# Gate and up weights of the second layer stored with their columns interleaved, and loaded with a stride

## The chip, the cores and the metric

The kernel runs on one core of one Trainium2 chip. The time is device microseconds of one execution, and the number compared is the median of several executions. TensorE does the matrix products: it loads 128 weight columns from SBUF and then streams a moving operand past them into PSUM. VectorE and ScalarE do elementwise work, SyncE issues most of the transfers.

## The reference, cut to what matters

One inference step of a two-layer decoder: 256 prompt tokens and 8 x 4 sample tokens share the weights, so 288 columns of activations in all. Each layer has a mixer (a retention and RG-LRU mixer in the first layer, an S5 state-space mixer with a GLU in the second) and then a SwiGLU feed-forward part:

```python
def swiglu(x, w_gu, w_down):
    h = x @ w_gu
    g, u = jnp.split(h, 2, axis=-1)
    return (jax.nn.silu(g) * u) @ w_down
...
            x = x + swiglu(rmsnorm(x, norm_ffn[layer]), w_ffn_gu[layer], w_ffn_down[layer])
```

`D_MODEL` is 2048 and `FFN_HIDDEN` 5632. All inputs are float32.

## The kernel before, in words

Activations lie with the 128 feature channels of a chunk on the partitions and the 288 tokens along the free dimension; 2048 features are 16 chunks. A weight matrix is stored by `_tiles` as tiles of 128 output columns: tile `t` is an array of 128 partitions by 2048, whose columns `128 k` to `128 k + 127` are the weights of chunk `k`.

The large products run in float32r. To keep accuracy, each float32 operand is split in two parts, a rounded one (`wh`, `xh`) and the rest (`wl`, `xl`), and each chunk takes three products: `wh` with `xh` (L328), `wh` with `xl` (L329), `wl` with `xh` (L330). Every product is one weight load (128 columns) and one pass over 288 columns of activations.

The program is a list of units, written out in order by `even_mixer`, `glu` and `ffn`. A `Unit` is one tile of output columns over the chunks `k0` to `k1`; `run_prog` plays the list. Each unit is cut in two halves, and each half (up to 8 chunks) has a weight slot of up to 1024 columns. For a slot, SyncE issues one transfer into `raw` (L274), ScalarE copies it to `wh` in float32r (L281), VectorE subtracts to get `wl` (L109, the helper of all tensor-tensor operations), and then TensorE runs the products of that half. There are four `raw` and four `wh` buffers, and three or four `wl` buffers, so these steps run ahead of TensorE by up to three slots. Chunk `k` is read as `wh[:, o:o + P]`, 128 neighbouring columns.

`ffn(l, ...)` takes the 44 tiles of the hidden width in three thirds, 0 to 14, 15 to 29 and 30 to 43 (`THIRDS`). In a third, each tile `t` has a gate unit and an up unit of 16 chunks each; then 16 units of the down projection follow. Gate and up results are evacuated from PSUM by VectorE and ScalarE (`evg`, `evu`). The activations of the second layer's feed-forward part are in the tiles `x` of the pool `x2`.

Other places that the text speaks of: L748 (`cross_sum`), products of 128 weight columns with 32 moving columns in float32; L533 (`lru_gate`), products with 312 moving columns in float32; and the VectorE operations of `yl_evac`, `gr_evac` and `rot_units`, where one operand (`hs` or `rot`) is read or written with a step of 4 elements for the prompt tokens, and in `yl_evac` with a step of 7 elements for the 32 sample tokens.

Of the kernel before, what the change touches and what calls it, by code (L numbers as in the profile page):

```python
# [19 lines left out]
P = 128  # L20
D = 2048
NT = D // P
# [7 lines left out]
NH = HID // P  # L30
# [10 lines left out]
V_BG = 96  # L41
V_CW, V_CB, V_BA, V_BX, V_LAM = 128, 160, 168, 176, 184
V_N = 192


@with_exitstack
def trunk_kernel(ctx: ExitStack, tc: tile.TileContext, ins, outs, upto=99, dbg=None):
    nc = tc.nc
    v, act, pe, pool, sp = nc.vector, nc.scalar, nc.tensor, nc.gpsimd, nc.sync
# [11 lines left out]
    def nm(s):  # L61
        cnt[0] += 1
        return f"{s}{cnt[0]}"

    def g_(w=N, p=P):
        return AP_["gen"].tile([P, TOK], F32, tag="g", name=nm("g"))[:p, :w]
# [24 lines left out]
    def mp_():  # L91
        return AP_["ps"].tile([P, 512], F32, tag="m", name=nm("mp"))
# [15 lines left out]
    def tt(o, a, b, op):  # L108
        v.tensor_tensor(o, a, b, op=op)  # L109
# [7 lines left out]
    def stt(o, a, s, b, op0, op1):  # L117
        v.scalar_tensor_tensor(o, a, s, b, op0=op0, op1=op1)
# [11 lines left out]

    vec = cst.tile([P, V_N], F32, name="vec")
    sp.dma_start(vec, ins["vec"])
# [12 lines left out]
    def later(n, fn):  # L145
        pend.append((step[0] + n, len(pend), fn))

    def run_due():
        due = [p for p in pend if p[0] <= step[0]]
        for p in due:  # L150
            pend.remove(p)
        for p in due:
            p[2]()
        if bgq:
            bg_one()
# [54 lines left out]
        return h, l  # L210

    class Unit:
        __slots__ = ("w", "k0", "k1", "rhs", "evac", "late")

        def __init__(self, w, k0, k1, rhs, evac, late=0):
            self.w, self.k0, self.k1, self.rhs, self.evac, self.late = w, k0, k1, rhs, evac, late

    prog = []
    S = {}
# [1 line left out]
    def unit(*a):  # L221
        prog.append(Unit(*a))

    def call(fn):
        prog.append(fn)

    def halves_of(u):
        m = u.k0 + (u.k1 - u.k0 + 1) // 2
        return [(u, u.k0, m), (u, m, u.k1)]

    def run_prog():
        ws, items, where, left = [], [], {}, []

        def slot(*pieces):
            o = 0
            for u, a, b in pieces:
                for k in range(a, b):
                    where[id(u), k] = (len(ws), a - o)
                o += b - a
            ws.append(pieces)  # L240
            left.append(o)
        lead = [u for u in prog if isinstance(u, Unit)][:4]
        for u in prog:
            if isinstance(u, Unit):
                if u in lead[1:]:
                    continue
                hs = [halves_of(x) for x in (lead if u is lead[0] else (u,))]
                for e in range(2):
                    for h in hs:
                        items.append(h[e])  # L250
                        slot(h[e])
            elif isinstance(u, tuple):
                for pieces in u[0]:
                    slot(*pieces)
                items.extend(u[1])
            else:
                items.append(u)
        accs = {}
        raws, whs, wls = {}, {}, {}
        S["whs"] = whs  # L260
        n = len(ws)
        LH, RAW = 3, 4
        for tag in ("raw", "wh"):
            wt.tile([P, 1024], F32R if tag == "wh" else F32, tag=tag, name=nm(tag))
        wt.tile([P, 32], F32, name="wpad", bufs=1)
        ring = [wt.tile([P, 1024], F32R, name=f"wl{k}", bufs=1) for k in range(3)]
        free = S["free"] = list(ring)
        size = [k * P for k in left]

        def dma(i):  # L270
            r = wt.tile([P, 1024], F32, tag="raw", name=nm("raw"), bufs=RAW)
            o = 0
            for u, a, b in ws[i]:
                sp.dma_start(r[:, o:o + (b - a) * P], u.w[:, a * P:b * P])  # L274
                o += (b - a) * P
            raws[i] = r

        def prep_h(i):
            w = size[i]
            wh = wt.tile([P, 1024], F32R, tag="wh", name=nm("wh"), bufs=LH + 1)  # L280
            act.activation(wh[:, :w], raws[i][:, :w], AF.Copy)  # L281
            whs[i] = wh

        def prep_l(i):
            w = size[i]
            wl = free.pop(0)
            tt(wl[:, :w], raws.pop(i)[:, :w], whs[i][:, :w].bitcast(F32), SUB)
            wls[i] = wl

        c = [0, 0, 0]  # L290
        done = 0

        def dma_next():
            dma(c[0])
            c[0] += 1

        def prep_next():
            prep_h(c[1])
            c[1] += 1

        def prepl_next():
            prep_l(c[2])
            c[2] += 1

        start(dma_next, prep_next, prepl_next)
        for h in items:
            while True:
                while c[0] < min(c[2] + RAW, n):
                    dma_next()
                while c[1] < min(c[0], done + LH + 1, n):  # L310
                    prep_next()
                if c[2] >= done + 3 or c[2] >= n:
                    break
                prepl_next()
            if not isinstance(h, tuple):
                h()
                continue
            u, a, b = h
            i, w0 = where[id(u), a]
            if a == u.k0:  # L320
                bank = mp_() if u in lead else psa.tile([P, 512], F32, tag="acc", name=nm("acc"))
                accs[id(u)] = (bank[:, :N], u.rhs())
            acc, rhs = accs[id(u)]
            wh, wl = whs[i], wls[i]
            for k in range(a, b):
                o = (k - w0) * P
                xh, xl = rhs[k - u.k0]
                pe.matmul(acc, lhsT=wh[:, o:o + P], rhs=xh, start=(k == u.k0), stop=False)  # L328
                pe.matmul(acc, lhsT=wh[:, o:o + P], rhs=xl, start=False, stop=False)  # L329
                pe.matmul(acc, lhsT=wl[:, o:o + P], rhs=xh, start=False, stop=(k == u.k1 - 1))  # L330
            if b == u.k1:
                if u in lead or u.late:
                    later(u.late or 3, lambda u=u, acc=acc: u.evac(acc))
                else:
                    u.evac(acc)
            left[i] -= b - a
            if left[i] == 0:
                whs.pop(i)
                free.append(wls.pop(i))
                assert i == done  # L340
                done += 1
                step[0] += 1
                run_due()
# [3 lines left out]
    xs = {}  # L347
# [603 lines left out]
    def ffn(l, fin):  # L951
        for a, b in THIRDS:
            hid = {}
            for t in range(a, b):
                st = {}

                def evg(ps, st=st):
                    g, t_ = g_(), g_()
                    tt(g, ps, rstd["v"], MUL)
                    act.activation(t_, g, AF.Tanh, scale=0.5)  # L960
                    st["g"], st["t"] = g, t_

                def evu(ps, st=st, t=t, hid=hid):
                    u = g_()
                    tt(u, ps, rstd["v"], MUL)
                    stt(st["g"], st["t"], 1.0, st["g"], ADD, MUL)
                    tt(u, u, st["g"], MUL)
                    hid[t] = split(u, 0.5, ac_, al_)
                late = 2 if t < 1 else 0
                unit(ins["w_gu"][l, t], 0, NT, lambda: xs["xg"], evg, late)  # L970
                unit(ins["w_gu"][l, NH + t], 0, NT, lambda: xs["xg"], evu, late)
            last = b == NH
            if last and l:
                call(lambda: act.preload_act_table_set("natural_log_exp_and_others"))
            for j in range(NT):
                unit(ins["w_dn"][l, j], a, b, lambda hid=hid, a=a, b=b: [hid[t] for t in range(a, b)],
                     res_evac(j, fin if last else None))
# [765 lines left out]
def _tiles(w):  # L1743
    k, m = w.shape[-2:]
    lead = w.shape[:-2]
    n = len(lead)
    w = w.reshape(*lead, k // P, P, m // P, P)
    return w.transpose(*range(n), n + 2, n + 1, n, n + 3).reshape(*lead, m // P, P, k)
# [6 lines left out]
def layout(i):  # L1755
    a = {k: np.asarray(x) for k, x in i.items()}
    o = dict(_consts())
    xp = a["x_prompt"].reshape(NCH, CH, D).transpose(2, 1, 0)
    xs = a["x_sample"].transpose(2, 1, 0)
# [6 lines left out]
    wo = a["w_out_even"][0]  # L1766
    o["w_out"] = _tiles(np.concatenate([wo[1024:], wo[:1024]], axis=0))
    o["w_gu"] = _tiles(a["w_ffn_gu"])
    o["w_dn"] = _tiles(a["w_ffn_down"])
    o["w_glu"] = _tiles(a["w_glu"][0])  # L1770
    o["lru_w"] = np.stack([a["lru_wa"][0], a["lru_wx"][0]]).reshape(2, 4, 2, P, P).transpose(1, 3, 2, 0, 4)
# [59 lines left out]
```

## Time and profile before

| | |
|---|---|
| median of 3 executions | 2468.62 us (2467.01 to 2472.24) |
| the profiled execution's own time | 2469.42 us |
| its span, first to last instruction | 2467.7 us |
| granted TensorE clock, mean | 0.995 |
| products at L328 to L330 | 5760 of each line |
| weights read by the gate and up transfers | 352 transfers of 512 KB |

The profile is one execution. PE is TensorE's products, PEld its weight loads, DVE VectorE, ACT ScalarE. The end of a product is modelled, and the rows of neighbouring products overlap, so the pace of products is read from their starts.

### The profile page before, as it was taken

The numbers are of one execution on the slowest core, as the hardware profiler recorded it, in microseconds if no ns is written. First come the engines' busy times: TensorE is split into PE (matmuls) and PEld (weight loads), VectorE is DVE, ScalarE is ACT, GpSimd is POOL, SyncE is SP. The second block draws the span as 40 slices with busy tenths as digits, with TensorE's granted clock in tenths as the row PEclk, the third lists the DMA queues.
The fourth block names the chain that finished last, engine by engine and source line by source line (L and its number), as shares of the span: only waits on it lengthen the run. The fifth ranks groups of instructions, "written<-read, shape, count | busy, mean of one in ns | idle before, by whom it ended". The sixth has DMA issues, their size and how long they took to land.

```text
span 2467.7 us, 49587 instructions
## 1 busy us (share of the span) xinstructions
PE 2426.4 (98%) x20130; PEld 2397.4 (97%) x20130; DVE 1636.6 (66%) x3033; ACT 1144.8 (46%) x1756; POOL 154.6 (6%) x299
## 2 busy tenths in 40 slices
PE   8999999999999999999999999999999999999997
PEld 8999999999999999999999899999999999999997
DVE  7767676677677878778856996655544555445554
ACT  6656554533355445455443554543333333333343
POOL 0111110000020121111110000000000000000000
PEclk9999999999999999999999999999999999999999
DMA  7656655555577777777788875555555555555553
GB/s 254 198 180 191 212 171 174 168 166 169 184 251 246 251 259 251 252 258 234 246 281 231 291 239 161 177 169 167 170 170 172 160 166 167 176 164 167 165 166 128
DMA packets 168612, 493.78 MB, mean 200 GB/s; under 512 B 30400, under 2 KB 42944, under 8 KB 168128
## 3 DMA queue, kind: packets, MB, share of 16 engines
q1 hardware_dynamic: 152192, 439.51, 56.2%
q0 software_dynamic: 15184, 49.77, 5.7%
q8 instruction: 159, 2.61, 0.4%
q10 hardware_dynamic: 1008, 1.33, 0.1%
q14 instruction: 69, 0.57, 0.1%
HBM read 449.16 MB, written 48.19 MB: 202 GB/s over the span
## 4 chain that ended last, share of the span: by engine, by line
PE 95%; DVE 2%; DMA 2%; issue 0%; ACT 0%; SPq 0%; DVEq 0%; ACTq 0%
PE acc L329 30%; PE acc L330 30%; PE acc L328 30%; DVE w L109 1%; PE po L1511 1%; DMA raw<-in_w_in_dram 1%; DVE wl L109 1%; PE pp L1448 0%; PE mp L788 0%; DMA raw<-in_w_dn_dram 0%; PE mp L533 0%; PE mp L1323 0%; PE mp L736 0%; DMA tab<-tabR 0%; PE mp L710 0%
## 5 line engine op out<-in xcount | busy, mean ns | idle before, releaser
L281 ACT ACTIVATE wh<-raw 128x1024 fp32r<-128x1024 f32 (+2 forms) x758 | 760.4, 1010 | 415.6 <-PE acc L329 262.4
L329 PE MATMUL acc<-xl,wh 128*128 128x288 f32 x2624 | 778.5, 297 | 0.0
L109 DVE TENSOR_TENSOR wl<-raw,wh 128x1024 fp32r<-128x1024 f32 (+3 forms) x601 | 697.0, 1172 | 23.0 <-ACT wh L281 15.7
L328 PE MATMUL acc<-xg,wh 128*128 128x288 f32 x2112 | 625.5, 296 | 0.0
L328 PE MATMUL acc<-ac,wh 128*128 128x288 f32 x2048 | 603.9, 295 | 2.2 <-ACT wh L281 1.2
L330 PE MATMUL acc<-xg,wl 128*128 128x288 f32 x1760 | 519.8, 295 | 0.0
L329 PEld LDWEIGHTS acc<-xl,wh 128*128 128x128 f32 x2624 | 494.0, 188 | 0.5
L330 PE MATMUL acc<-ac,wl 128*128 128x288 f32 x1610 | 476.3, 296 | 3.5 <-DVE wl L109 3.0
L329 PE MATMUL acc<-al,wh 128*128 128x288 f32 x1568 | 465.9, 297 | 0.0
L329 PE MATMUL acc<-x,wh 128*128 128x288 f32 x1408 | 418.2, 297 | 0.0
L328 PE MATMUL acc<-x,wh 128*128 128x288 f32 x1408 | 412.1, 293 | 0.0
L328 PEld LDWEIGHTS acc<-xg,wh 128*128 128x128 f32 x2112 | 398.1, 188 | 1.7 <-issue 0.8
L328 PEld LDWEIGHTS acc<-ac,wh 128*128 128x128 f32 x2048 | 386.1, 189 | 4.7 <-ACT wh L281 1.4
L330 PEld LDWEIGHTS acc<-xg,wl 128*128 128x128 f32 x1760 | 330.5, 188 | 0.1
L330 PE MATMUL acc<-x,wl 128*128 128x288 f32 x1056 | 309.9, 293 | 0.0
L109 DVE TENSOR_TENSOR g<-acc,rstd 128x288 f32<-128x288 f32 x192 | 87.7, 457 | 334.5 <-PE acc L330 333.9
L330 PEld LDWEIGHTS acc<-ac,wl 128*128 128x128 f32 x1610 | 303.1, 188 | 6.2 <-DVE wl L109 6.2
L329 PEld LDWEIGHTS acc<-al,wh 128*128 128x128 f32 x1568 | 295.3, 188 | 0.0
L328 PEld LDWEIGHTS acc<-x,wh 128*128 128x128 f32 x1408 | 264.7, 188 | 0.1
L329 PEld LDWEIGHTS acc<-x,wh 128*128 128x128 f32 x1408 | 264.0, 188 | 0.1
L109 DVE TENSOR_TENSOR X<-X,acc 128x288 f32<-128x288 f32 x112 | 50.8, 453 | 229.6 <-PE acc L330 229.3
L330 PEld LDWEIGHTS acc<-x,wl 128*128 128x128 f32 x1056 | 198.4, 188 | 0.0
(311 smaller groups left out, 2620.2 us busy)
## 6 DMA issues: line engine op xcount, KB each, us to landing
raw<-in_w_gu_dram SPq DMA_DIRECT2D x352, 512.0 KB, 4.7
raw<-in_w_dn_dram SPq DMA_DIRECT2D x128, 448.0 KB, 4.3
raw<-in_w_in_dram SPq DMA_DIRECT2D x96, 512.0 KB, 4.5
raw<-in_w_dn_dram SPq DMA_DIRECT2D x64, 512.0 KB, 3.7
raw<-in_w_out_dram SPq DMA_DIRECT2D x32, 512.0 KB, 4.1
raw<-in_w_glu_dram SPq DMA_DIRECT2D x40, 384.0 KB, 4.4
raw<-in_w_glu_dram SPq DMA_DIRECT2D x32, 320.0 KB, 3.9
out_ret_s_dram<-s POOLq DMA_DIRECT2D x16, 512.0 KB, 4.5
```

What stands on the lines that cost most here:

```text
L109: v.tensor_tensor(o, a, b, op=op)
L281: act.activation(wh[:, :w], raws[i][:, :w], AF.Copy)
L328: pe.matmul(acc, lhsT=wh[:, o:o + P], rhs=xh, start=(k == u.k0), stop=False)
L329: pe.matmul(acc, lhsT=wh[:, o:o + P], rhs=xl, start=False, stop=False)
L330: pe.matmul(acc, lhsT=wl[:, o:o + P], rhs=xh, start=False, stop=(k == u.k1 - 1))
L1511: pe.matmul(po[32 * q:32 * q + 32, t * NC:t * NC + NC], lhsT=r[:, c0:c0 + 32], rhs=H[:, ri, q, :NC], start=False, stop=(t == CH - 1 and ri ...
```

## The change

The host stores the gate and up tiles of the second layer in another order of columns, and the products read it back with a step. `mixed(t)` is the number of chunks whose columns are interleaved: 1 (as before) for tiles 0 to 7, 8 for tiles 8 to 14, 2 for tiles 15 to 29, 4 for tiles 30 to 43. In a group of `n` chunks, column `c` of chunk `i` lies at place `n c + i`, and the load takes 128 columns that are `n` elements apart. Both `wh` and `wl` are read so, since they are made from the slot as it lies. Every engine has the same instructions in the same order as before; only the pattern of 3456 weight loads differs (672 with a step of 8 elements, 1440 with 2, 1344 with 4), and the contents of the tiles in memory.

```diff
--- before.py
+++ after.py
@@ -43,6 +43,10 @@
 V_N = 192
 
 
+def mixed(t):
+    return 1 if t < 8 else 8 if t < 15 else 2 if t < 30 else 4
+
+
 @with_exitstack
 def trunk_kernel(ctx: ExitStack, tc: tile.TileContext, ins, outs, upto=99, dbg=None):
     nc = tc.nc
@@ -210,10 +214,10 @@
         return h, l
 
     class Unit:
-        __slots__ = ("w", "k0", "k1", "rhs", "evac", "late")
-
-        def __init__(self, w, k0, k1, rhs, evac, late=0):
-            self.w, self.k0, self.k1, self.rhs, self.evac, self.late = w, k0, k1, rhs, evac, late
+        __slots__ = ("w", "k0", "k1", "rhs", "evac", "late", "mix")
+
+        def __init__(self, w, k0, k1, rhs, evac, late=0, mix=1):
+            self.w, self.k0, self.k1, self.rhs, self.evac, self.late, self.mix = w, k0, k1, rhs, evac, late, mix
 
     prog = []
     S = {}
@@ -323,11 +327,12 @@
             acc, rhs = accs[id(u)]
             wh, wl = whs[i], wls[i]
             for k in range(a, b):
-                o = (k - w0) * P
+                g, i_ = divmod(k - w0, u.mix)
+                o = slice(g * P * u.mix + i_, (g + 1) * P * u.mix, u.mix)
                 xh, xl = rhs[k - u.k0]
-                pe.matmul(acc, lhsT=wh[:, o:o + P], rhs=xh, start=(k == u.k0), stop=False)
-                pe.matmul(acc, lhsT=wh[:, o:o + P], rhs=xl, start=False, stop=False)
-                pe.matmul(acc, lhsT=wl[:, o:o + P], rhs=xh, start=False, stop=(k == u.k1 - 1))
+                pe.matmul(acc, lhsT=wh[:, o], rhs=xh, start=(k == u.k0), stop=False)
+                pe.matmul(acc, lhsT=wh[:, o], rhs=xl, start=False, stop=False)
+                pe.matmul(acc, lhsT=wl[:, o], rhs=xh, start=False, stop=(k == u.k1 - 1))
             if b == u.k1:
                 if u in lead or u.late:
                     later(u.late or 3, lambda u=u, acc=acc: u.evac(acc))
@@ -967,8 +972,8 @@
                     tt(u, u, st["g"], MUL)
                     hid[t] = split(u, 0.5, ac_, al_)
                 late = 2 if t < 1 else 0
-                unit(ins["w_gu"][l, t], 0, NT, lambda: xs["xg"], evg, late)
-                unit(ins["w_gu"][l, NH + t], 0, NT, lambda: xs["xg"], evu, late)
+                unit(ins["w_gu"][l, t], 0, NT, lambda: xs["xg"], evg, late, mixed(t) if l else 1)
+                unit(ins["w_gu"][l, NH + t], 0, NT, lambda: xs["xg"], evu, late, mixed(t) if l else 1)
             last = b == NH
             if last and l:
                 call(lambda: act.preload_act_table_set("natural_log_exp_and_others"))
@@ -1766,6 +1771,9 @@
     wo = a["w_out_even"][0]
     o["w_out"] = _tiles(np.concatenate([wo[1024:], wo[:1024]], axis=0))
     o["w_gu"] = _tiles(a["w_ffn_gu"])
+    for t in range(2 * NH):
+        n = mixed(t % NH)
+        o["w_gu"][1, t] = o["w_gu"][1, t].reshape(P, NT // n, n, P).transpose(0, 1, 3, 2).reshape(P, D)
     o["w_dn"] = _tiles(a["w_ffn_down"])
     o["w_glu"] = _tiles(a["w_glu"][0])
     o["lru_w"] = np.stack([a["lru_wa"][0], a["lru_wx"][0]]).reshape(2, 4, 2, P, P).transpose(1, 3, 2, 0, 4)
```

## Rows read from the trace of the kernel before

**Rows 1.** The page: busy time of each engine, and the chain that ended last.

```profile
PE 2426.4 (98%) x20130; PEld 2397.4 (97%) x20130; DVE 1636.6 (66%) x3033; ACT 1144.8 (46%) x1756; POOL 154.6 (6%) x299
...
PE 95%; DVE 2%; DMA 2%; issue 0%; ACT 0%; SPq 0%; DVEq 0%; ACTq 0%
```

**Rows 2.** Timeline, PE, second layer's gate and up: start us, us, engine, line, operation.

```profile
1700.06 0.29 PE L328 MATMUL acc<-x,wh 128*128 128x288 f32 x1
1700.19 0.30 PE L329 MATMUL acc<-x,wh 128*128 128x288 f32 x1
1700.32 0.29 PE L330 MATMUL acc<-x,wl 128*128 128x288 f32 x1
1700.45 0.29 PE L328 MATMUL acc<-x,wh 128*128 128x288 f32 x1
```

**Rows 3.** Windows, PE: the stretches of tiles 8-14, 15-29, 30-43; one unit.

```profile
core 0: us, PE busy (x), PEclk, DMA share, GB/s
1722.48:1810.59 88.11, 88.11 (x675) 1.00 0.52 167
1904.99:2093.77 188.78, 188.78 (x1442) 1.00 0.53 167
2188.19:2364.40 176.21, 176.21 (x1347) 1.00 0.52 166
...
1904.99:1911.28 6.29, 6.29 (x51) 1.00 0.57 199
```

**Rows 4.** Groups by form, 1904.99 to 2093.77 us: busy us, mean ns, idle before.

```profile
L281 ACT ACTIVATE wh<-raw 128x1024 fp32r<-128x1024 f32 x59 | 62.1, 1053 | 26.0 <-PE acc L329 18.2 <-ACT wh L281 4.2 <-issue 3.6
L109 DVE TENSOR_TENSOR wl<-raw,wh 128x1024 fp32r<-128x1024 f32 x45 | 53.5, 1217 | 0.0
L109 DVE TENSOR_TENSOR wlx<-raw,wh 128x1024 fp32r<-128x1024 f32 x14 | 17.2, 1225 | 4.6 <-ACT wh L281 4.6
```

**Rows 5.** Timeline, 91.98 to 92.60 us, around line 748.

```profile
91.99 0.53 PEld L748 LDWEIGHTS mp<-e_eye,g 128*128 128x128 f32 x4
...
92.11 0.53 PE L748 MATMUL mp<-e_eye,g 128*128 128x32 f32 x4
...
92.44 0.19 PEld L328 LDWEIGHTS acc<-xg,wh 128*128 128x128 f32 x1
```

**Rows 6.** Timeline, PE, 61.5 to 64.3 us, around line 533.

```profile
62.15 2.26 PE L533 MATMUL mp<-l,lw 128*128 128x312 f32 x8
64.25 0.27 PE L776 MATMUL mp<-ident,g 128*96 128x128 f32 x1
```

**Rows 7.** Windows, PE: one gate unit of the first layer.

```profile
768.12:774.52 6.40, 6.40 (x50) 1.00 0.85 266
```

**Rows 8.** Groups by form, DVE: contiguous, then one operand strided.

```profile
L109 DVE TENSOR_TENSOR px<-pw,pb 128x256 f32<-128x256 f32 x128 | 48.1, 416 | 0.0
...
L109 DVE TENSOR_TENSOR rot<-g,g 128x256 f32<-128x256 f32 x16 | 9.3, 617 | 0.0
...
L109 DVE TENSOR_TENSOR R<-rt,rt 128x256 f32<-128x256 f32 x16 | 6.0, 415 | 0.0
...
L109 DVE TENSOR_TENSOR g<-g,rot 128x256 f32<-128x256 f32 x8 | 5.0, 623 | 0.3
...
L109 DVE TENSOR_TENSOR g<-g,hs 128x256 f32<-128x256 f32 x8 | 5.0, 622 | 0.3
...
L109 DVE TENSOR_TENSOR g<-g,hs 128x32 f32<-128x32 f32 x8 | 1.7, 210 | 0.0
...
L109 DVE TENSOR_TENSOR g<-g,rot 128x32 f32<-128x32 f32 x8 | 1.5, 186 | 0.0
```

**Rows 9.** Windows, all engines, start of the S5 mixer: us, busy, granted clock.

```profile
1340.00:1360.00 20.00, 17.21 (x367) 15.98 (x367) 18.00 (x39) 4.39 (x14) 0.72 (x2) 0.83 0.72 213
...
1400.00:1440.00 40.00, 39.12 (x817) 36.71 (x816) 39.66 (x69) 22.60 (x56) 1.59 (x5) 1.00 0.90 310
```

## The prediction

> **What bounds the kernel now.** I began with the page's chain of work that ended last and the busy shares: TensorE holds 95% of the chain and is busy for 98% of the span [rows 1]. That busy share is no measure of pace, since a product's row of about 0.29 us overlaps the next; pace is read from starts. In the timeline of the second layer's gate and up products, the same line comes back every 0.39 us, and three products lie between, so one takes 0.131 us [rows 2]. Over whole stretches: the gate and up products of tiles 8 to 14, 15 to 29 and 30 to 43 take 88.11, 188.78 and 176.21 us at a granted clock of 1.00, that is 2.4 GHz [rows 3]. A tile has a gate and a up unit, each 16 chunks by 3 products, so 96 products a tile: 672, 1,440 and 1,344, and 453.10 us / 3,456 = 131.1 ns each.
>
> Nothing else sets the pace there. ScalarE's copy into `wh` waits for TensorE to give a buffer back, and VectorE's subtraction into `wl` has no idle time before it except for ScalarE; both are done well inside the 6.29 us of a unit: two ScalarE rows of 1,053 ns and two VectorE rows of 1,217 ns [rows 4]. So time added to or taken from a product there goes to the end one for one.
>
> What a product needs: the moving operand, 288 columns, and a fresh load of 128 weight columns, which overlaps the product before it. Two places show these apart. *The load*: at line 748 four products of only 32 columns follow one another; the loads start at 91.99 us and the next line's load at 92.44, so a load that nothing hides takes 0.45/4 = 112.5 ns, 0.88 ns a column [rows 5]. *The stream*: at line 533 eight products of 312 columns start at 62.15 and the next line at 64.25, 262.5 ns each, 0.84 ns a column [rows 6]. Those are float32; the float32r products here take 131.1/288 = 0.455 ns a column, so they stream at about twice that rate, which I estimate as 288 x 0.42 = 121 ns. Today the load (112.5) hides under the stream (121), and about 10 ns on top belong to neither. They depend on where the operands lie: layer 0's unit from 768.12 to 774.52 us, same shapes and clock, takes 133.3 ns a product against 131.0 [rows 3, 7].
>
> **The change, part by part.** No instruction is added, removed or moved on any engine, and no transfer changes size: a weight slot still is 1,024 contiguous columns (512 KB). DMA, the copy and the subtraction run over whole slots and do not see the order of columns: zero. What changes is the reading pattern of 3,456 weight loads: columns 4 bytes apart become 8 bytes apart (1,440 loads, tiles 15 to 29), 16 (1,344, tiles 30 to 43) or 32 (672, tiles 8 to 14). Tiles 0 to 7 stay.
>
> No load of before reads with a stride, so its price must be bounded. The nearest rows are VectorE's, also 4-byte elements out of SBUF, at a rate like the load's. Its additions and products over 256 contiguous elements take 415 and 416 ns; the same operation with one input read 16 bytes apart (`hs`, `rot`) takes 622 and 623 ns, with the output written so 617 [rows 8]. That is (622 - 416)/256 = 0.80 ns more for each element. At 28 bytes apart, over 32 elements, it is 210 against 186, 0.75 ns more: the price does not grow from 16 bytes up [rows 8].
>
> *Strides 4 and 8 (2,016 loads).* With 0.80 ns more a column the load takes 112.5 + 128 x 0.80 = 215 ns. It no longer hides under the 121 ns stream; it paces the products, as at line 748. Per product 215 - 131 = 84 ns, times 2,016 = **+169 us**. Bounds: from below, if the load grows by the ratio of the whole instructions, 622/416, it takes 168 ns, +37 x 2,016 = +75 us. From above, VectorE's slope between 32 and 256 strided elements is (622 - 210)/224 = 1.84 ns; at that a load takes 235 ns, +104 x 2,016 = +210 us. I take the middle since it adds the extra that was measured to the load that was measured. The lowest ends are in the rivals.
>
> *Stride 2 (1,440 loads).* No row reads 8 bytes apart. If the price belongs to opening a fresh 16-byte piece at 1.84 ns, two columns share one and a load takes 64 x 1.84 = 118 ns, still under 131: zero. If half the 0.80 ns were paid, 164 ns, +33 x 1,440 = +47 us. The other end is the gain of rival 2, -14 us. I take **zero**, since the opened piece fits the equal price at 16 and 28 bytes.
> The Trainium skill (Advanced Engine Details and Errata, SBUF Cachelines) says that SBUF has 16-byte lines and needs two hits on a line for full speed, which by that rule leaves stride 2 free and gives the same sum; no run here shows it for TensorE.
>
> *The clock.* A paced product streams for 121 of 215 ns. Where TensorE last ran thinly, 1340 to 1360 us, with PE busy 17.21 of 20 us, the granted clock was 0.83 [rows 9]; from 1400, with 39.12 of 40, it was 1.00. If it fell to 1.2 GHz, the stream would take 242 ns and pace instead: +27 x 2,016 = +54 us more. Rows of busy time will still look full, so I take zero and keep +54 for the range.
>
> Sum: the profiled execution took 2469.4 us (span 2467.7), 0.8 above the median of the runs shown; 2469.4 + 169 = **2638 us**.
>
> **Rivals.**
> 1. *The load does not care about stride: no change, 2469 us.* A load may fetch its columns otherwise than VectorE, with more in flight; it has 131 - 112 = 19 ns to spare, so up to 0.14 ns a column would stay hidden, a sixth of VectorE's price. Against it: two inputs and an output on VectorE all paid alike, which looks like the memory and not the engine.
> The Trainium skill (TensorE: Matmul & The Clock Gate, LDWEIGHTS) gives the load's time by the number of columns alone, as columns / 1.2 GHz, an estimate of 107 ns for 128; by that rule the change is worth nothing, and line 748's 112.5 ns agrees for contiguous columns only.
> 2. *Faster: 2435 to 2455 us.* The 10 ns between 121 and 131.1 move with addresses [rows 3, 7], as if reads of load and stream got in each other's way in SBUF. A stream takes about two columns for each that the load takes; read two apart, the load would pass through SBUF at the stream's speed, and the two might stay clear of each other. Price: at most 10.1 ns x 3,456 = -35 us if all strides do it, 10.1 x 1,440 = -14.5 us if only stride 2 does. It decides where the strided load stays below 121 ns. Against it: the starts in the timeline are 0.13 us apart without exception [rows 2], and a wider stride touches more of SBUF.
> 3. *Slightly slower, about 2504 us.* The loads stay hidden, but touching two to four times as much of SBUF doubles the 10 ns: +10 x 3,456 = +35 us.
>
> **How the numbers follow.** Forecast 0.60, rival 1 0.15, rival 2 0.14, rival 3 0.11. A difference below 0.2% (5 us) can't be told from none here. So faster 0.14, same 0.15, slower 0.71. The forecast's own range, with its bounds and the clock, is 2544 to 2700 us; the whole range goes on to rivals 3 and 1, 2460 to 2700, and leaves out rival 2 and a case where stride 2 pays as well and the clock falls (together about 0.2).
>
> **What would show it.** By step: tiles 0 to 7 keep 131 ns a product; tiles 8 to 14 take 672 x 215 = 144 us instead of 88; tiles 30 to 43, 289 instead of 176; tiles 15 to 29 stay at 189. TensorE's starts would be 0.64 us apart for three products, ScalarE and VectorE would idle longer on TensorE, and the granted clock would stay 1.00. The forecast is wrong if strides 4 and 8 pace differently from each other, if all three stay near 131 ns (rival 1), if stride 2 falls towards 121 (rival 2), or if all rise alike by some 10 ns (rival 3).

## The result, and the profile after

The changed kernel takes 2688.34 us (median of 4 runs, 2688.13 to 2689.32) against 2470.20 us (median of 4) of the kernel before: a ratio of 1.0889, with a 95% interval of 1.0876 to 1.0902. The profiled execution took 2688.37 us with a span of 2686.6 us, 218.9 us more than before.

The windows of TensorE in the profile of the changed kernel, over tiles 0 to 7 (step 1), 8 to 14 (step 8), 15 to 29 (step 2) and 30 to 43 (step 4); columns: stretch, its length, busy time with the number of products, granted clock, DMA share, GB/s:

```profile
core 0: us, PE busy (x), PEclk, DMA share, GB/s
1621.71:1722.90 101.19, 101.19 (x772) 1.00 0.53 168
1722.90:1885.98 163.08, 163.08 (x674) 1.00 0.28 91
1980.38:2172.38 192.00, 192.00 (x1442) 1.00 0.52 164
2266.78:2583.36 316.58, 316.58 (x1346) 1.00 0.30 93
```

Against [rows 3], tiles 8 to 14 grew by 163.08 - 88.11 = 74.97 us, tiles 30 to 43 by 316.58 - 176.21 = 140.37, tiles 15 to 29 by 192.00 - 188.78 = 3.22. That is 218.56 of the 218.9 us, and tiles 0 to 7 took 101.19 us in both profiles, so the rest of the program took the same time to within 0.4 us. Per product: step 8 takes 163.08/672 = 242.7 ns, step 4 takes 316.58/1344 = 235.6, step 2 takes 192.00/1440 = 133.3, against 131.1 before.

The chain of waits and the busy shares say almost the same as before [rows 1], though the kernel lost 9%:

```profile
PE 2644.4 (98%) x20130; PEld 2615.8 (97%) x20130; DVE 1637.5 (61%) x3033; ACT 1144.9 (43%) x1756; POOL 154.1 (6%) x299
...
PE 96%; DVE 2%; DMA 1%; issue 0%; ACT 0%; DVEq 0%; SPq 0%; ACTq 0%
```

VectorE and ScalarE did the same work in the same time; only TensorE's rows grew. A busy share of 98% covers a product of 131 ns as well as one of 236. The first pointer to the cause is the weight loads' own rows. The groups by form, tiles 30 to 43, of the kernel before and then of the changed one (count, busy us, mean ns of one):

```profile
L328 PEld LDWEIGHTS acc<-x,wh 128*128 128x128 f32 x448 | 84.2, 188 | 0.0
L329 PEld LDWEIGHTS acc<-x,wh 128*128 128x128 f32 x448 | 84.0, 188 | 0.0
```

```profile
L334 PEld LDWEIGHTS acc<-x,wh 128*128 128x128 f32 x448 | 148.7, 332 | 0.0
L333 PEld LDWEIGHTS acc<-x,wh 128*128 128x128 f32 x448 | 148.3, 331 | 0.0
```

The same loads, of the same shapes (L328 and L329 are L333 and L334 in the changed kernel), have rows of 332 ns where they had 188, and the shape in the row (128x128) does not tell that the columns now lie 16 bytes apart. A row is longer than what its load costs (188 ns, where [rows 5] gives 112.5 for a load that nothing hides), and the products' own rows grew as well, so the price and the cause are read from the starts and from the experiments. The starts in the timeline of the changed kernel are 0.235 us apart where [rows 2] has 0.13:

```profile
2299.99 0.40 PE L333 MATMUL acc<-x,wh 128*128 128x288 f32 x1
2300.22 0.40 PE L334 MATMUL acc<-x,wh 128*128 128x288 f32 x1
2300.46 0.40 PE L335 MATMUL acc<-x,wlx 128*128 128x288 f32 x1
```

### The profile page after: what moved, and what is told of

Its sections match the earlier page's. It is cut to its first block, busy times and chain, and to the rows that moved or that the text cites. A ratio compares the mean times of both kernels' runs of the same rounds, so it can differ in the third digit from the quotient of the medians.

```text
span 2686.6 us, 49587 instructions
## 1 busy us (share of the span) xinstructions
PE 2644.4 (98%) x20130; PEld 2615.8 (97%) x20130; DVE 1637.5 (61%) x3033; ACT 1144.9 (43%) x1756; POOL 154.1 (6%) x299
## 4 chain that ended last, share of the span: by engine, by line
PE 96%; DVE 2%; DMA 1%; issue 0%; ACT 0%; DVEq 0%; SPq 0%; ACTq 0%
PE acc L334 31%; PE acc L335 30%; PE acc L333 30%; DVE w L113 1%; PE po L1516 1%; DVE wl L113 0%; PE pp L1453 0%; DMA raw<-in_w_glu_dram 0%; PE mp L334 0%; PE mp L793 0%; PE mp L335 0%; PE mp L333 0%; PE mp L538 0%; PE mp L1328 0%; PE mp L741 0%
## 5 line engine op out<-in xcount | busy, mean ns | idle before, releaser
L334 PE MATMUL acc<-xl,wh 128*128 128x288 f32 x2624 | 778.5, 297 | 0.0
L333 PE MATMUL acc<-xg,wh 128*128 128x288 f32 x2112 | 625.5, 296 | 0.0
L333 PE MATMUL acc<-ac,wh 128*128 128x288 f32 x2048 | 604.0, 295 | 2.2 <-ACT al L1615 1.1
L334 PEld LDWEIGHTS acc<-xl,wh 128*128 128x128 f32 x2624 | 494.0, 188 | 0.5
L334 PE MATMUL acc<-x,wh 128*128 128x288 f32 x1408 | 488.4, 347 | 0.0
L333 PE MATMUL acc<-x,wh 128*128 128x288 f32 x1408 | 485.7, 345 | 0.0
L334 PE MATMUL acc<-al,wh 128*128 128x288 f32 x1568 | 465.9, 297 | 0.0
L113 DVE TENSOR_TENSOR g<-acc,rstd 128x288 f32<-128x288 f32 x192 | 87.8, 457 | 552.9 <-PE acc L335 552.4
L333 PEld LDWEIGHTS acc<-xg,wh 128*128 128x128 f32 x2112 | 398.1, 188 | 1.7 <-issue 0.8
L333 PEld LDWEIGHTS acc<-ac,wh 128*128 128x128 f32 x2048 | 386.2, 189 | 4.6 <-ACT wh L285 1.3
L335 PE MATMUL acc<-x,wl 128*128 128x288 f32 x1056 | 366.1, 347 | 0.0
L334 PEld LDWEIGHTS acc<-x,wh 128*128 128x128 f32 x1408 | 365.9, 260 | 0.1
L333 PEld LDWEIGHTS acc<-x,wh 128*128 128x128 f32 x1408 | 365.1, 259 | 0.1
L334 PEld LDWEIGHTS acc<-al,wh 128*128 128x128 f32 x1568 | 295.3, 188 | 0.0
L335 PEld LDWEIGHTS acc<-x,wl 128*128 128x128 f32 x1056 | 275.4, 261 | 0.0
```

The costliest lines, as they stand in the source:

```text
L333: pe.matmul(acc, lhsT=wh[:, o], rhs=xh, start=(k == u.k0), stop=False)
L334: pe.matmul(acc, lhsT=wh[:, o], rhs=xl, start=False, stop=False)
L335: pe.matmul(acc, lhsT=wl[:, o], rhs=xh, start=False, stop=(k == u.k1 - 1))
```

## The experiments

Three questions were open after the result. Is it really the load that paces, and by what measure (lines opened, a threshold, a distance)? Why 235 ns and not the 215 I had summed? And what are the 10 ns that I could give to neither load nor stream? The theory on record (A) is that a load pays about 1.84 ns, VectorE's slope from [rows 8], for each 16-byte piece of SBUF that it opens. All runs below but "step 2 everywhere" were executed once, and the pace of a product is read from a window of their traces.

**All steps from 1 to 8.** The weights stay in their old order, and each group of tiles reads with another step:

```diff
 def mixed(t):
-    return 1 if t < 8 else 8 if t < 15 else 2 if t < 30 else 4
+    return 1 + t // 5 if t < 30 else 7 if t < 37 else 8
...
-                g, i_ = divmod(k - w0, u.mix)
-                o = slice(g * P * u.mix + i_, (g + 1) * P * u.mix, u.mix)
+                i_ = (k - w0) % u.mix
+                o = slice((k - w0) * P, (k - w0 + 1) * P) if u.mix == 1 else slice(i_, i_ + 127 * u.mix + 1, u.mix)
```

> The second layer's gate and up weights are stored as before; their loads read with a step of 1 element for tiles 0 to 4, 2 for 5 to 9, 3 for 10 to 14, 4 for 15 to 19, 5 for 20 to 24, 6 for 25 to 29, 7 for 30 to 36 and 8 for 37 to 43, from the first elements of the slot, so the products there take the wrong weights; the amount of work is the same. Theory A, lines: a load pays about 1.84 ns for each 16-byte piece of SBUF that it opens, and a product takes the longer of that and its 131 ns. Steps 1 and 2 (32 and 64 pieces): 131 and 133 ns a product; step 3 (96 pieces): 177 ns; steps 4 to 8 (128 pieces each): 235 to 243 ns. Rival C, threshold: a step under 16 bytes is free, step 3 takes 131 to 133 ns, steps 4 to 8 235 to 243. Rival D, distance: the price grows with the step, so 4 to 8 rise one after another by more than 10 ns in all.

One tile (96 products) for each step from 1 to 8, windows of TensorE:

```profile
1646.53:1659.12 12.59, 12.59 (x99) 1.00 0.56 170
1709.89:1722.69 12.80, 12.80 (x99) 1.00 0.53 165
1782.10:1799.00 16.90, 16.90 (x97) 1.00 0.38 125
1974.04:1996.65 22.61, 22.61 (x97) 1.00 0.28 93
2085.44:2107.23 21.79, 21.79 (x98) 1.00 0.31 97
2194.64:2216.56 21.92, 21.92 (x97) 1.00 0.30 96
2401.43:2423.93 22.50, 22.50 (x97) 1.00 0.29 93
2583.84:2607.15 23.31, 23.31 (x97) 1.00 0.28 90
```

Divided by 96: 131, 133, 176, 236, 227, 228, 234 and 243 ns. Step 3 decides. Its 128 columns lie 12 bytes apart, on 96 pieces of 16 bytes, and 96 x 1.84 = 177. So there is no threshold at 16 bytes (rival C: 131 to 133). From step 4 on each column has a piece of its own and the price stays within 227 to 243. It falls by 9 ns from step 4 to step 5, so it does not rise from step to step as rival D would have it; but it then rises by 16 ns from step 5 to step 8, and no run explains that spread, so a small price for distance is not excluded. The three steps of the changed kernel came out as in its own stretches, on weights in the old order, so which weights lie where does not matter.

**Short streams.** The changed kernel, with most products cut to 64 (gate units) or 160 columns (up units) of activations:

```diff
+                if u.cut and 0 < k < u.k1 - 1:
+                    for l_, r_ in ((wh, xh), (wh, xl), (wl, xh)):
+                        pe.matmul(acc[:, :u.cut], lhsT=l_[:, o], rhs=r_[:, :u.cut], start=False, stop=False,
+                                  skip_group_check=True)
+                    continue
...
```

> The changed kernel, but in the second layer's gate and up units chunks 1 to 14 stream only the first 64 columns (gate) or 160 columns (up) of the activations; the rest of those columns gets only chunks 0 and 15. The loads are as in the change. Theory A, the load alone paces: in 64-column products step 1 takes 112 ns, step 2 118, steps 4 and 8 235 to 243 as with 288 columns; with 160 columns the same. Rival B, load and stream collide: alone a load with step 4 or 8 takes the 215 ns of my prediction and the other 20 to 28 ns come from the stream, so 64-column products fall to 215 ns and those of 160 columns lie between. For step 1, 160 columns take under 121 ns either way.

Windows of 42 cut products each: step 1 and step 2 with 64 columns, step 4 with 64 and with 160, step 1 with 64 again at a lower clock:

```profile
1620.42:1625.02 4.60, 4.60 (x44) 1.00 0.12 48
2012.27:2017.12 4.85, 4.85 (x44) 1.00 0.47 150
2458.84:2468.51 9.67, 9.67 (x43) 0.50 0.32 110
2470.12:2479.90 9.78, 9.78 (x43) 0.50 0.35 107
...
1649.41:1658.23 8.82, 8.82 (x44) 0.50 0.37 121
```

Divided by 42: 110, 115, 230 and 233 ns. Step 2 alone takes 115, near 64 pieces x 1.84 = 118, and that is why it hides. The two windows of step 4 ran at a granted clock of 0.50 (1.2 GHz), so they can't be set beside the changed kernel's 236 ns at 1.00 without more. Near the start of tile 30, nine gaps between products of 64 columns, with step 4, still ran at 1.00:

```profile
2391.08:2393.19 2.11, 2.11 (x12) 1.00 0.12 43
```

That is 2.11/9 = 234 ns with a stream of 64 columns against 236 with 288, at the same clock. Rival B, that load and stream collide and a load alone would take 215, falls: the load alone paces.

I had not expected the clock: in this run of short streams the granted clock was 0.50 in most of the gate and up part. There a contiguous load takes 8.82/42 = 210 ns, nearly twice its time. A load with step 2 takes 210 as well, where it took 115 (42 products again):

```profile
2028.62:2037.43 8.81, 8.81 (x43) 0.50 0.38 119
```

A load with step 4 takes at 0.50 what it takes at 1.00. So the numbers fit a load that takes the longer of two times: that of its columns, which follows TensorE's clock (110 and 210 ns), and that of its pieces, which does not (234 and 230 to 233).

**Fewer weight columns.** Old order, 288 columns of stream; eight chunks of each gate unit load another number of columns:

```diff
+LOADS = ((128, 4), (96, 4), (64, 4), (32, 4), (128, 1), (64, 1), (64, 8))
...
+                        pe.matmul(acc[:m_], lhsT=l_[:, :(m_ - 1) * s_ + 1:s_], rhs=r_, start=False, stop=False,
+                                  skip_group_check=True)
```

> In the second layer's gate units chunks 4 to 11 load fewer or strided weight columns, tile by tile in turn: 128, 96, 64 and 32 columns with step 4, 128 and 64 with step 1, 64 with step 8; the output rows above are left out there and the weights taken are the wrong ones. The stream of 288 columns stays. Theory A, 1.84 ns for each piece: 128 with step 4 takes 235 ns a product, 96 takes 177, 64 (118 ns) and 32 hide and take 131, 64 with step 8 takes 131, the contiguous ones 131. Rival, a strided load pays a fixed sum of 104 ns over its 0.88 ns a column: 96 columns 189 ns, 64 columns 160 ns, with step 8 as well, 32 columns 132.

Windows of 24 products: 128, 96, 64 and 32 columns with step 4, 128 with step 1, 64 with step 8:

```profile
1714.70:1720.35 5.65, 5.65 (x26) 1.00 0.41 114
1729.80:1734.04 4.24, 4.24 (x26) 1.00 0.25 58
1743.64:1746.83 3.19, 3.19 (x27) 1.00 0.07 10
1756.43:1759.60 3.17, 3.17 (x27) 1.00 0.12 16
1769.04:1772.19 3.15, 3.15 (x27) 1.00 0.08 9
...
1794.18:1797.40 3.22, 3.22 (x26) 1.00 0.07 8
```

That is 235, 177, 133, 132, 131 and 134 ns. The price goes by pieces; a fixed sum for a strided load would have left 64 columns at 160. With 64 columns the load takes less than the stream and hides again.

**Step 2 everywhere**, timed:

```diff
 def mixed(t):
-    return 1 if t < 8 else 8 if t < 15 else 2 if t < 30 else 4
+    return 2
```

> The changed kernel with 2 for all 44 tiles: the whole gate and up part of the second layer reads with step 2. From the stretch of tiles 15 to 29 of the changed kernel (192.00 us against 188.78, +2.2 ns a product) I expect +2.2 x 4224 = +9 us against before, ratio 1.004. Rival: step 2 is free and those 3 us had another cause in that stretch: ratio 1.000.

2481.57 us against 2469.81, ratio 1.0046 (1.0034 to 1.0058): 11.8 us, about the 9 expected. So the small price of step 2 is real: 11.8 us are 2.8 ns a product, and the interval (2.0 to 3.4) holds the 2.2 of the stretch.

**Where the reads begin.** The start of each load is shifted from tile to tile, for step 1 and step 2:

```diff
+SHIFT = [4 * i for i in range(16)] + [1, 2, 3, 5, 6, 7]
...
+    step, d = 1 + (m - 1) // 22, SHIFT[(m - 1) % 22]
+    o = d + P * step * (i % (7 if step == 1 else 3))
+    return w[:, o:o + (P - 1) * step + 1:step]
```

> Weights stored as before; tiles 0 to 21 load contiguous columns, tiles 22 to 43 columns with step 2, and in each of the two sets the start of the read is moved by 0, 4, 8, ... 60 elements (16-byte steps over 256 bytes) and then 1, 2, 3, 5, 6, 7 elements, one shift a tile; the products take the wrong weights, the amount of work is the same. Theory of the prediction's second rival, collisions of load and stream by address: the pace of a product moves with the shift, by 3 ns or more between the best and the worst of a set, and somewhere comes near 121 ns. Rival: the 10 ns over the stream are fixed, every contiguous tile takes 131 ns and every step-2 tile 133.

First single tiles (step 1, shifts of 16 and 28 bytes; step 2, shifts of 96 and 112 bytes), then all tiles of step 1 in two stretches (0 to 14, 15 to 21) and all of step 2 (22 to 29, 30 to 43):

```profile
1635.15:1648.05 12.89, 12.89 (x98) 1.00 0.60 187
...
1984.44:1997.03 12.59, 12.59 (x99) 1.00 0.49 156
2073.55:2086.38 12.83, 12.83 (x98) 1.00 0.53 164
2086.38:2099.11 12.73, 12.73 (x98) 1.00 0.50 159
```

```profile
1622.07:1813.60 191.53, 191.53 (x1444) 1.00 0.52 165
1908.01:1997.03 89.02, 89.02 (x675) 1.00 0.51 165
1997.03:2099.11 102.08, 102.08 (x770) 1.00 0.52 166
2193.51:2372.81 179.30, 179.30 (x1346) 1.00 0.52 164
```

The pace moves with the shift, from 12.59/96 = 131.1 ns to 12.89/96 = 134.3, but none comes near 121, so my second rival has no case. Over all shifts step 1 takes (191.53 + 89.02)/2112 = 132.8 ns and step 2 (102.08 + 179.30)/2112 = 133.2. Most of the 2.2 ns of step 2 is therefore a matter of place: the kernel before lies at one of the best shifts for step 1, and the changed kernel's place is an average one for step 2. Which bits of the address decide was not settled.

**What paces when the load does not.** Eight chunks of each gate unit stream other parts of the activations past contiguous loads:

```diff
+MOVING = ((288, 1), (256, 1), (224, 1), (144, 2), (128, 2), (72, 4), (64, 4))
...
+                        pe.matmul(acc[:, :n_], lhsT=l_[:, o], rhs=r_[:, :(n_ - 1) * s_ + 1:s_], start=False, stop=False,
+                                  skip_group_check=True)
```

> Contiguous loads as before; in the second layer's gate units chunks 4 to 11 stream another part of the activations: tile by tile in turn 288, 256 or 224 neighbouring columns, 144 or 128 columns with step 2, 72 or 64 columns with step 4. What they would have added to the other columns is left out. Theory A extended: the stream, too, pays about 1.82 ns for each 16-byte piece it opens, and that is why a product takes 131 and not 121 ns. A product takes the longest of the pieces' time, the clock's time for its columns and the load's 112 ns: 288, 144 with step 2 and 72 with step 4 (72 pieces each) all 131 to 133 ns; 256, 128 with step 2 and 64 with step 4 (64 pieces) 116 to 121 ns; 224 columns (56 pieces, 102 ns) 112 ns. Rival, the 10 ns are collisions of load and stream: 144, 128, 72 and 64 columns need 60 ns or less by the clock, so all four take the load's 112 ns.

Windows of 24 products: 288, 256 and 224 columns, 144 and 128 with step 2, 72 with step 4.

```profile
1715.81:1718.96 3.15, 3.15 (x27) 1.00 0.09 9
1728.40:1731.22 2.82, 2.82 (x26) 1.00 0.01 4
1740.67:1743.34 2.67, 2.67 (x27) 1.00 0.00 2
1752.79:1755.92 3.13, 3.13 (x27) 1.00 0.10 9
1765.39:1768.14 2.75, 2.75 (x26) 1.00 0.00 0
1777.61:1780.21 2.60, 2.60 (x27) 1.00 0.00 2
```

131, 118, 111, 130, 115 and 108 ns (64 columns with step 4 took 108 as well). This is a half miss. 144 columns with step 2 take as long as 288 contiguous ones, as the extended theory said and the clock does not explain; but 72 columns with step 4 open as many pieces and hide under the load. To see the stream alone, the same products then loaded only 32 columns (diff against that last run):

```diff
-MOVING = ((288, 1), (256, 1), (224, 1), (144, 2), (128, 2), (72, 4), (64, 4))
+MOVING = ((288, 1), (256, 1), (144, 2), (128, 2), (96, 3), (72, 4), (36, 8))
...
-                        pe.matmul(acc[:, :n_], lhsT=l_[:, o], rhs=r_[:, :(n_ - 1) * s_ + 1:s_], start=False, stop=False,
+                        pe.matmul(acc[:32, :n_], lhsT=l_[:, o.start:o.start + 32], rhs=r_[:, :(n_ - 1) * s_ + 1:s_], start=False, stop=False,
```

> As the run with other moving operands, but chunks 4 to 11 of the second layer's gate units load only 32 contiguous weight columns (about 28 ns by line 748's 0.88 ns a column), so that the stream alone paces; the rows of output above 32 are left out there. Tile by tile in turn the stream is 288 or 256 neighbouring columns, 144 or 128 with step 2, 96 with step 3, 72 with step 4, 36 with step 8. Theory A extended, 1.82 ns for each 16-byte piece of the stream: 131, 117, 131, 117, 131, 131 and 66 ns a product. Rival, the stream runs by the clock (0.42 ns a column) and only a load beside it makes it slower: 121, 108, 61, 54, 41, 31 and under 31 ns. Third, from the run before, where 72 columns with step 4 hid under the load's 112 ns while 144 with step 2 did not: steps 1 and 2 as the extended theory, step 4 under 112 ns.

Windows of 24 products, in the order of the list:

```profile
1703.81:1706.96 3.15, 3.15 (x27) 1.00 0.17 49
1716.55:1719.33 2.78, 2.78 (x26) 1.00 0.00 0
1728.77:1731.87 3.10, 3.10 (x27) 1.00 0.03 3
1741.35:1744.11 2.76, 2.76 (x26) 1.00 0.04 13
1753.57:1755.67 2.10, 2.10 (x27) 1.00 0.01 6
1765.14:1766.74 1.60, 1.60 (x26) 1.00 0.08 33
1776.27:1777.06 0.79, 0.79 (x27) 1.00 0.31 124
```

131, 116, 129, 115, 88, 67 and 33 ns. The stream of 288 contiguous columns takes 131 ns even with next to no load beside it: collisions with the load are not what the 10 ns are. Per column the contiguous streams take 0.456 and 0.453 ns, the others 0.90, 0.90, 0.91, 0.93 and 0.92, whatever the step. So the stream does not pay by 16-byte pieces; the numbers fit one read of SBUF each 0.91 ns that yields two neighbouring columns or one strided one. That reading fits all seven, but no run looked into the reads themselves. The clock gives it one more support. In the run with short streams, whole products of 288 columns came at a granted clock of 0.50, five gaps in this window:

```profile
1658.61:1659.81 1.20, 1.20 (x6) 0.50 0.00 0
```

That is 240 ns, 0.83 ns a column, and half of it would be 120. At 1.00 the stream takes 131, so there something other than the clock holds it.

No version here that does the whole work beats the kernel before. Contiguous loads hide under a stream that takes 131 ns by itself, so a better order of weights has nothing left to gain in these products.

## Why the prediction was right, and where a term was off

*What bounds.* TensorE set the end there, one for one: the three stretches give 218.56 of 218.9 us, and ScalarE, VectorE and the transfers only waited longer (VectorE's wait for TensorE before `g<-acc,rstd` went from 334.5 to 552.9 us). Right.

*Strides 4 and 8.* The mechanism held: a load of 112.5 ns that hides becomes one that paces. The size was off. I forecast +84 ns a product and +169 us, and measured 104.5 ns (step 4) and 111.6 ns (step 8), +215.3 us. The step that failed is the choice between the bounds, "I take the middle since it adds the extra that was measured to the load that was measured". A strided column does not pay 0.80 ns on top of the load's 0.88; it costs 1.84 ns in all, on TensorE as on VectorE, so the upper bound, 128 x 1.84 = 235 ns, was the price itself. [Rows 8] could have told: on VectorE the contiguous element costs (416 - 186)/224 = 1.03 ns by my estimate, so 0.80 is what is missing from 1.03 to 1.84, and on a load that starts from 0.88 the same 0.80 ends at 1.68. Step 8 is 7 ns above 235, and steps 5 and 6 are 7 to 8 below; that spread is open. The prediction had named it as a sign of being wrong "if strides 4 and 8 pace differently from each other": they do, by 7 ns, so the equal price from 16 bytes up holds only to some 3%.

*The range* held partly by luck. With the upper bound alone it would have ended at 2469.4 + 210 = 2679 us, below the measured 2688.34. It reached 2700 by its other allowances, the clock's above all (+54 on the forecast is 2692), and the clock did not fall.

*Stride 2.* Forecast zero, measured +3.2 us. The reason given was right (two columns share a piece: 115 ns alone, hidden), and the rest is a matter of place. Here the Trainium skill (Advanced Engine Details and Errata, SBUF Cachelines) agrees with the runs: two hits on a 16-byte line are enough, 115 ns, and one is not, 234.

*The 10 ns that "belong to neither"* were mine to misread: I put the stream at 121 ns from line 533's rate, and it is 131. Line 533's float32 products advance a column in 0.84 ns, and the float32r stream is not twice as fast but 0.456. The forecast's sum did not hang on it; the prices of rivals 2 and 3 did, and both had nothing to give or to double.

*Rival 1*, a load whose time goes by its number of columns alone, is out: 128 columns took between 110 and 243 ns at a granted clock of 1.00. The rule of the Trainium skill (TensorE: Matmul & The Clock Gate, LDWEIGHTS), an estimate of 107 ns from the number of columns, nearly holds here for steps 1 and 2 (110 and 115 ns), and not for steps 3 to 8 (176 to 243). *Rival 3*, all stretches alike by 10 ns, is out. *The clock* stayed at 1.00 in the changed kernel, as forecast, with products that pace at 236 and stream for 131.

## What to carry to other kernels

Before giving a weight load a step, count the 16-byte pieces of SBUF that it will open, and look for a strided operation of another engine in the same trace: VectorE's 1.84 ns an element priced TensorE's loads to within a few per cent. A moving operand goes by another count: every step tried doubled the price of a column. Take such a price as the whole cost of an element where it is a rate, and not as something added to the contiguous cost. A load that hides is free only up to the time of the stream over it, so judge a change of layout by starts of products, not by busy shares, which read 98% before and after.

## What was not expected of the hardware

- A load with step 4 does not follow TensorE's clock: 230 to 234 ns at a granted 0.50 and at 1.00, while the contiguous load went from 110 to 210 ns, and the load with step 2 from 115 to 210.
- A float32r stream is held to about 0.456 ns a column (131 ns for 288) at a granted clock of 1.00, even beside a load of 32 columns, and to 0.90 to 0.93 ns a column with a step of 2, 3, 4 or 8.
- In the run with products of 64 or 160 columns, paced by their loads, the granted clock was 0.50 for most of the gate and up part; the changed kernel's products, paced by their loads as well but with 288 columns, kept 1.00.
